# High and low activation parts as one 512-column moving operand in 39 projection units

## The chip, the cores and the metric

The kernel runs on one core of one Trainium2 chip. The metric is the device time of one execution in microseconds (us); three runs of the kernel before have a median of 1357.82 us (1357.82 to 1359.32).

## What is computed

The reference is two transformer-like blocks over 256 tokens of width 1024, in float32. Only the parts that the change touches are shown:

```python
# first block
h = rms_norm(x, g_pre_mix) * (1 + scale1) + shift1
(sc_b, sc_c, sc_x, q, k, v, z, xbc, dt_raw, gl_a, gl_b, gl_c) = split_columns(h @ w_in)
y_a = short_conv_mixer(sc_b, sc_c, sc_x, sc_conv_w) @ w_sc_out      # conv(sc_c * sc_x) * sc_b
y_b = stick_breaking_attention(q, k, v) @ w_sb_out
y_c = mamba2_mixer(z, xbc, dt_raw, ...) @ w_ssm_out                 # conv over xbc, then a scan
merged = sigmoid(gl_a) * y_a + sigmoid(gl_b) * y_b + sigmoid(gl_c) * y_c
x = x + gate1 * rms_norm(merged @ w_o, g_post_mix)
gt, up = jnp.split(h2 @ w_ffn_in, 2, axis=-1)
f = (silu(gt) * up) @ w_ffn_out
# second block
q, k, v, u = jnp.split(h @ w_in, ...)     # dilated attention on q, k, v; pooling on u
x = x + g1 * (concat([attn, pool]) @ w_out)
x = x + g2 * peer_ffn(h2, ...)            # 16384 experts, all evaluated densely here
```

## The kernel before, in words

**Split arithmetic.** Every projection multiplies weights by activations in a 32-bit format of reduced precision (`fp32r`). Both operands are split in a high part and the rest, and a product is the sum of three: weight high by activation high, weight high by activation low, weight low by activation high (`mm3`, lines 378 to 381). The activations stand in `hh` and `hl`, 8 chunks (k) of 128 channels by 256 tokens each.

**A unit.** Weights come in units of 1 MB (256 output columns): one DMA into a tile `raw`, then for each of the two halves s of 128 columns ScalarE casts the high part (`h`, line 148) and VectorE subtracts to get the low part (`l`, line 149). `raw`, `h` and `l` each have three buffers and a fourth that every fourth tile takes, so a load waits until VectorE has read the tile that held its buffer. `fm_steps` (line 383 on) runs a unit: for each half 8 chunks of three matmuls, 48 in all, each with 256 moving columns, into one PSUM tile of the tag `mm` that holds both halves. There are two `mm` tiles, which all units share in turn. The caller then evicts both halves at once: the gate columns with a ScalarE copy (line 631), `sc_c` with a ScalarE copy (line 658), q, k and u of the second block with ScalarE copies (lines 985, 988, 997); the feed-forward with a silu on ScalarE and a multiplication on VectorE that read PSUM (lines 935 and 936).

**Other work on VectorE and ScalarE.** Beside the units run a conditioning product with the weights `mod_w` and `w_ada` (VectorE, line 171, two instructions of 1024 columns for a load of 1 MB; `side()` hands one load to each unit of the first stage), in the first block the convolution of `xbc` (`conv`, lines 614 and 617, six chunks), the short convolution, both mixers, and in the second block the pooling and the softmax (`scores`). Every engine works through its instructions in a fixed order, which a scheduler sets when the program is built. The code steers it with `tc.issue_after(ins)`: what is written under it comes after `ins`. `hold["gate"]` keeps the eviction of the last unit for that purpose:

```python
    sc_c()
    with tc.issue_after(hold["gate"].ins):
        conv(4)
    ...
    with tc.issue_after(hold["gate"].ins):
        conv(0)
    sc_x()
    with tc.issue_after(hold["gate"].ins):
        conv(2)
```

**Stages of the program**, with their times in the trace: input projection by chunks to 65 us; v, `sc_c`, `sc_x` and 12 gate units woven with the mixers (the gate stage) to 203.8 us; `w_o` and a norm to 248 us; the feed-forward (10 steps of two input units and one output unit) to 424 us; a norm; u, q, k and scores of the second block from 445.6 to 485 us; attention and `w_out` to 518 us; then the dense expert part to the end, which uses `fm_steps` and is not rewritten.

Of the kernel before, what the change touches and what calls it, by code (L numbers as in the profile page):

```python
# [7 lines left out]
F32 = mybir.dt.float32  # L8
F32R = mybir.dt.float32r
# [4 lines left out]
AF = mybir.ActivationFunctionType  # L14
ALU = mybir.AluOpType
# [26 lines left out]
def kernel(ctx: ExitStack, tc: tile.TileContext, a: dict, out: bass.AP):  # L42
    nc = tc.nc
    mm = nc.tensor.matmul
    V, S, G = nc.vector, nc.scalar, nc.gpsimd

    const = ctx.enter_context(tc.tile_pool(name="const", bufs=1))
    pers = ctx.enter_context(tc.tile_pool(name="pers", bufs=1))
# [56 lines left out]
    cb = {}  # L105
    modp = {}

    def load_c(i, pool, tag="cb"):
        cb[i] = pool.tile([P, D], F32, tag=tag, name=f"cb{i}{tag}")
        src = a["c_2" if i else "c"]  # L110
        nc.sync.dma_start(cb[i], bass.AP(tensor=src.tensor, offset=src.offset, ap=[[0, P], [1, D]]))
        S.activation(cb[i], cb[i], AF.Silu)
# [208 lines left out]
    def residual_norm(acc, gb, normed, affine, xt, name, ws):  # L321


        got = []
        hh = pers.tile([P, KC, T], F32R, tag="hh", name="hh" + name)
        hl = pers.tile([P, KC, T], F32R, tag="hl", name="hl" + name)
        scale, shift = affine
        def start(c):
            gm[c], rn[c] = gated(c, acc[c], gb, normed, "r" + name, xt[c])
# [162 lines left out]
    for hs in HALF:  # L492
        pt = mmtile(f"pc{hs.start}")
        mm(pt, ones1[0:1, :], crow[:, hs], start=True, stop=True)
        with tc.issue_after(sq.ins):
            S.activation(cb[0][:, hs], pt, AF.Silu)
    hh = pers.tile([P, KC, T], F32R, tag="hh", name="hhn1")
    hl = pers.tile([P, KC, T], F32R, tag="hl", name="hln1")
    coef = work.tile([P, 8], F32, tag="cf", name="cf1", bufs=4)
    acc = [t.rearrange("p (s t) -> p s t", s=2) for t in  # L500
           [mmtile(f"acc_j{n}") for n in range(2)] + [attile(f"acc_i{n}") for n in range(6)]]
# [123 lines left out]
    sgs = {}  # L625

    def gate_unit(n):
        b, u = divmod(n, 4)
        if u == 0:
            sgs[b] = w1.tile([P, KC, T], F32, tag="sg", name=f"sg{b}", bufs=2)  # L630
        hold["gate"] = S.copy(sgs[b][:, 2 * u:2 * u + 2], fm_unit(W, 2 + n, hh, hl, f"gl{b}{u}"))

    def branch(b, src, yh, yl, kn):
        S.activation(sgs[b], sgs[b], AF.Sigmoid)
# [20 lines left out]
    scc = w1.tile([P, 2, T], F32, name="scc")  # L655

    def sc_c():
        hold["gate"] = S.copy(scc, fm_unit(W, 0, hh, hl, "scc"))

    def sc_x():  # L660
        hold["gate"] = V.tensor_tensor(upad[:, :, 2:], fm_unit(W, 1, hh, hl, "scx"), scc, op=ALU.mult)
# [252 lines left out]
    for u in range(11):  # L914
# [11 lines left out]
            continue  # L926
        fh = r2(f"fh{u}")
        for k in range(2):
            pt = fm_unit(a["w_ffn_in"], 2 * u + k, hh, hl, f"fi{u}{k}")
            for _ in range(1 + (k == 1 and u in (3, 6))):  # L930
                with after(u - 1):
                    mod_run()
                mod_load(*next(mods))
            sl = w0.tile([P, T], F32, tag="sl", name=f"sl{u}{k}", bufs=2)
            S.activation(sl, pt[:, 0], AF.Silu)
            later_than[u] = V.tensor_tensor(fh[:, k], pt[:, 1], sl, op=ALU.mult)
        if u == 1:
            pt = attile("pft").rearrange("p (k t) -> p k t", k=2)
            for c in range(2):
# [42 lines left out]
    cat = w2.tile([P, KC, T], F32, tag="cat", name="cat")  # L982

    def q_unit(u):
        S.copy(qf[:, 2 * u:2 * u + 2], fm_unit(W, u, hh, hl, f"q2{u}"))

    def k_unit(u):
        S.copy(kf[:, 2 * u:2 * u + 2], fm_unit(W, 2 + u, hh, hl, f"k2{u}"))

    def v_units():  # L990
        pv = [mmtile(f"pv2{c}") for c in range(2)]
# [2 lines left out]
            S.copy(vf[:, c], pv[c])  # L994

    def up_unit(u):
        S.copy(up[:, 2 * u:2 * u + 2, 16:], fm_unit(W, 4 + u, hh, hl, f"u2{u}"))


    es, pos = {}, {}  # L1000
# [309 lines left out]
    woven(1, range(NU - NB, NU), v_steps)  # L1310
    b4.close()
    more.update(pool=ctx.enter_context(tc.tile_pool(name="more2", bufs=1)), tags=("wh", "wl"))
    fin = pers.tile([P, 2, D], F32, tag="hl", name="fin")
    gb, fg = fin[:, 0], fin[:, 1]
    load_c(1, pers, "hh")
    S.dma_start(fg, bass.AP(tensor=a["final_g_2"].tensor, offset=a["final_g_2"].offset, ap=[[0, P], [1, D]]))
    for u in range(32, 62):
        if u in (33, 36, 39, 42):
# [8 lines left out]
    v_unit(62, 63)  # L1327


    gm = pers.tile([P, 2, D], F32, tag="hh", name="gm")  # L1330
    for c in range(2):
        o = gm[:, c]
        gated(c, acc[c], gb, False, "ry", None, o)
# [92 lines left out]
```

## Time and profile before

| | |
|---|---|
| runs, median of 3 | 1357.82 us |
| profiled execution, its own time | 1358.11 us |
| span of its trace | 1356.1 us |
| TensorE clock granted, mean | 0.989 |
| TensorE (PE) busy | 1309.2 us, 97% |
| VectorE (DVE) busy | 1032.9 us, 76% |
| ScalarE (ACT) busy | 651.2 us, 48% |
| HBM read | 281 MB |

In the rows that follow, PE is TensorE's matmuls, PEld its weight loads, DVE VectorE, ACT ScalarE, POOL GpSimd, SPq the queue that starts most DMAs. L149 is line 149 of the kernel before. A tile is named after the unit: `pgl` is the PSUM tile of a gate unit, `hgl` and `lgl` the high and low parts of its weights, `rgl` the loaded tile; `pscc` and `pscx` are the PSUM tiles of `sc_c` and `sc_x`; `pfi`, `hfi`, `lfi` belong to the feed-forward input. A busy time of a matmul is longer than its share of the array, since matmuls are pipelined; the distance between starts is what counts.

### The profile page before, as it was taken

The page shows a single profiled execution, that of the slowest core. Times are in us where ns is not written, and L with a number is a line of the kernel's source. Part 1 is how long each engine was busy: PE and PEld are TensorE (multiplying, and loading weights), DVE is VectorE, ACT ScalarE, POOL GpSimd, SP SyncE. Part 2 cuts the span into 40 slices and gives each one's busy share as a digit, 9 for nine tenths or more (in the row PEclk, how much of TensorE's full clock was granted, in tenths as well). Part 3 has the DMA queues.
Part 4 walks back from the last instruction along what each step waited for, and adds up shares of the span by engine and source line. Part 5 has one row for each costly group of instructions (what it writes and reads, how often), then busy time and mean ns, then how long its engine had stood idle before and what let it go on. Part 6 is the DMA issues. An engine that isn't in the chain of part 4 may idle for free.

```text
span 1356.1 us, 23558 instructions
## 1 busy us (share of the span) xinstructions
PE 1309.2 (97%) x9601; PEld 1200.8 (89%) x9601; DVE 1032.9 (76%) x1908; ACT 651.2 (48%) x838; POOL 121.9 (9%) x109
## 2 busy tenths in 40 slices
PE   7999998999998999998999999999999999999996
PEld 6999997999996988998999999999998888888885
DVE  6899876787986885758858688886447999865555
ACT  5576554544444564444445433434444443445443
POOL 0000002000002002544442000000000000000001
PEclk9999998999999999999999999999999999999999
DMA  8866574888875542444445544444555444676551
GB/s 346 341 249 249 220 268 150 308 321 338 334 305 233 188 170 97 157 178 151 152 176 185 187 156 156 164 170 168 186 190 213 160 182 156 239 261 229 186 188 60
DMA packets 41454, 283.64 MB, mean 209 GB/s; under 512 B 5041, under 2 KB 5377, under 8 KB 8194
## 3 DMA queue, kind: packets, MB, share of 16 engines
q1 hardware_dynamic: 40768, 281.12, 56.0%
q8 instruction: 75, 1.23, 0.4%
q10 hardware_dynamic: 578, 1.02, 0.2%
q14 instruction: 33, 0.27, 0.1%
HBM read 281.03 MB, written 1.09 MB: 208 GB/s over the span
## 4 chain that ended last, share of the span: by engine, by line
PE 85%; DVE 8%; ACT 3%; POOL 2%; issue 1%; DMA 0%; POOLq 0%; SPq 0%; ACTq 0%; DVEq 0%
PE acc_y L431 25%; PE pU L379 8%; PE pU L381 8%; PE pU L380 8%; PE acc_f L431 4%; PE pfi L380 3%; PE pfi L381 3%; PE pfi L379 3%; PE pw L1157 2%; PE pgl L379 1%; PE pgl L381 1%; PE pgl L380 1%; PE acc L431 1%; PE acc_o L431 1%; DVE mod L171 1%
## 5 line engine op out<-in xcount | busy, mean ns | idle before, releaser
L381 PE MATMUL pU<-hhn,lU 128*128 128x256 f32 x1024 | 291.1, 284 | 6.4 <-DVE lU L149 5.8
L379 PE MATMUL pU<-hhn,hU 128*128 128x256 f32 x1024 | 293.9, 287 | 1.9 <-ACT g L1121 1.0
L380 PE MATMUL pU<-hln,hU 128*128 128x256 f32 x1024 | 290.4, 284 | 0.0
L148 ACT CAST hU<-rU 128x1024 fp32r<-128x1024 f32 x128 | 133.9, 1049 | 212.7 <-PE pU L380 179.6
L148 ACT CAST hV<-rV 128x1024 fp32r<-128x1024 f32 x128 | 134.8, 1053 | 195.7 <-PE acc_y L431 151.8
L149 DVE TENSOR_TENSOR lV<-rV,hV 128x1024 fp32r<-128x1024 f32 x128 | 156.5, 1223 | 89.2 <-ACT hV L148 89.2
L149 DVE TENSOR_TENSOR lU<-rU,hU 128x1024 fp32r<-128x1024 f32 x105 | 131.7, 1256 | 98.1 <-ACT hU L148 98.1
L381 PEld LDWEIGHTS pU<-hhn,lU 128*128 128x128 f32 x1024 | 197.0, 192 | 7.6 <-DVE lU L149 6.6
L431 PE MATMUL acc_y<-hV,hP 128*128 128x512 f32 x512 | 202.0, 395 | 0.0
L431 PE MATMUL acc_y<-hV,lP 128*128 128x512 f32 x512 | 199.6, 390 | 0.0
L379 PEld LDWEIGHTS pU<-hhn,hU 128*128 128x128 f32 x1024 | 197.0, 192 | 2.6 <-ACT g L1121 1.2
L431 PE MATMUL acc_y<-lV,hP 128*128 128x512 f32 x512 | 199.3, 389 | 0.0
L380 PEld LDWEIGHTS pU<-hln,hU 128*128 128x128 f32 x1024 | 197.2, 193 | 0.3
L431 PEld LDWEIGHTS acc_y<-lV,hP 128*128 128x128 f32 x512 | 96.1, 188 | 19.9
L431 PEld LDWEIGHTS acc_y<-hV,lP 128*128 128x128 f32 x512 | 96.3, 188 | 18.9 <-DVE lP L375 0.4
L431 PEld LDWEIGHTS acc_y<-hV,hP 128*128 128x128 f32 x512 | 96.2, 188 | 18.9
L379 PE MATMUL pfi<-hhn,hfi 128*128 128x256 f32 x320 | 90.6, 283 | 0.0
L380 PE MATMUL pfi<-hln,hfi 128*128 128x256 f32 x320 | 90.5, 283 | 0.0
L381 PE MATMUL pfi<-hhn,lfi 128*128 128x256 f32 x320 | 90.5, 283 | 0.0
L148 ACT CAST hfi<-rfi 128x1024 fp32r<-128x1024 f32 x43 | 45.1, 1050 | 54.5 <-PE pfi L380 20.8
L149 DVE TENSOR_TENSOR lfi<-rfi,hfi 128x1024 fp32r<-128x1024 f32 x43 | 52.0, 1223 | 24.3 <-ACT hfi L148 24.2
L379 PEld LDWEIGHTS pfi<-hhn,hfi 128*128 128x128 f32 x320 | 61.4, 192 | 0.4
(538 smaller groups left out, 2869.8 us busy)
## 6 DMA issues: line engine op xcount, KB each, us to landing
rU<-in_peer_u_dram SPq DMA_DIRECT2D x64, 1024.0 KB, 4.8
rV<-in_peer_v_dram SPq DMA_DIRECT2D x64, 1024.0 KB, 4.8
mod<-in_mod_w_dram SPq DMA_DIRECT2D x24, 1024.0 KB, 6.0
mod<-in_w_ada_dram SPq DMA_DIRECT2D x24, 1024.0 KB, 5.0
rfi<-in_w_ffn_in_dram SPq DMA_DIRECT2D x22, 1024.0 KB, 7.3
rgl<-in_w_in_dram SPq DMA_DIRECT2D x12, 1024.0 KB, 4.8
rfo<-in_w_ffn_out_dram SPq DMA_DIRECT2D x11, 1024.0 KB, 8.3
rwq<-in_peer_wq_dram SPq DMA_DIRECT2D x8, 1024.0 KB, 4.9
```

Of the source, the lines that this page charges most:

```text
L148: S.copy(h, r)
L149: hold["l"] = (G if pool_lo and s else V).tensor_tensor(l, r, h.bitcast(F32), op=ALU.subtract)
L171: V.scalar_tensor_tensor(t[:, s], t[:, s], 1.0, cb[i], op0=ALU.mult, op1=ALU.mult, accum_out=mod[:, i, n:n + 1])
L379: mm(o, wh, ah, start=start, stop=False, skip_group_check=skip)
L380: mm(o, wh, al, start=False, stop=False, skip_group_check=skip)
L381: mm(o, wl, ah, start=False, stop=stop, skip_group_check=skip)
L431: mm(acc[c][b], st[:, k, tk], w[:, HALF[b]], start=start and k == 0 and n == 0, stop=stop and k == 1 and n == 2)
L1157: mm(pw[:, t], oa[:, q, :, r], og[:, i, q, :, r], start=(i == 0), stop=(i == 1))
```

## The change

`hh` and `hl` become the two halves of one tile `hw` of [128, 8, 2, 256]. A new function `fm_sums` takes the place of `fm_steps` in 39 units: 12 gate units, `sc_c`, 20 feed-forward input units, and two each of q, k and u. For each half and chunk it issues one matmul of 512 moving columns (weight high by activation high and low side by side) and one of 256 (weight low by activation high), 32 matmuls a unit. Each half has an `mm` tile of its own: its columns 256 to 511 hold weight high by activation low, columns 0 to 255 the sum of the other two products. To evict a half, ScalarE copies columns 256 to 511 to the destination in SBUF, and VectorE adds columns 0 to 255 to it. `hold["gate"]` is now that addition. `sc_x` and the expert part keep `fm_steps`. The feed-forward evicts into a tile `fp` and applies silu and the multiplication there. The last buffers (`fin`, `gm`, the second use of `cb`) move into the tag `hw`.

```diff
+    def fm_sums(src, u, dst, name, pool_lo=False):
+        side()
+        for s, h, l in weights(src, u, name, pool_lo):
+            pt = mmtile(f"p{name}{s}")
+            h = h.rearrange("p (k n) -> p k n", k=KC)
+            l = l.rearrange("p (k n) -> p k n", k=KC)
+            for k in range(KC):
+                def wide(stop):
+                    mm(pt, h[:, k], hw["t"][:, k].rearrange("p z t -> p (z t)"), start=k == 0, stop=stop,
+                       skip_group_check=True)
+
+                if k == 0:
+                    wide(False)
+                mm(pt[:, :T], l[:, k], hw["t"][:, k, 0], start=False, stop=False, skip_group_check=True)
+                if k:
+                    wide(k == KC - 1)
+            S.copy(dst[:, s], pt[:, T:])
+            hold["gate"] = V.tensor_tensor(dst[:, s], pt[:, :T], dst[:, s], op=ALU.add)
+            yield s
...
-        hold["gate"] = S.copy(sgs[b][:, 2 * u:2 * u + 2], fm_unit(W, 2 + n, hh, hl, f"gl{b}{u}"))
+        list(fm_sums(W, 2 + n, sgs[b][:, 2 * u:2 * u + 2], f"gl{b}{u}"))
...
-        hold["gate"] = S.copy(scc, fm_unit(W, 0, hh, hl, "scc"))
+        list(fm_sums(W, 0, scc, "scc"))
...
-            pt = fm_unit(a["w_ffn_in"], 2 * u + k, hh, hl, f"fi{u}{k}")
+            pt = r2(f"fp{u}{k}")
+            list(fm_sums(a["w_ffn_in"], 2 * u + k, pt, f"fi{u}{k}"))
...
-            sl = w0.tile([P, T], F32, tag="sl", name=f"sl{u}{k}", bufs=2)
-            S.activation(sl, pt[:, 0], AF.Silu)
-            later_than[u] = V.tensor_tensor(fh[:, k], pt[:, 1], sl, op=ALU.mult)
+            S.activation(pt[:, 0], pt[:, 0], AF.Silu)
+            later_than[u] = V.tensor_tensor(fh[:, k], pt[:, 1], pt[:, 0], op=ALU.mult)
...
-        S.copy(qf[:, 2 * u:2 * u + 2], fm_unit(W, u, hh, hl, f"q2{u}"))
+        list(fm_sums(W, u, qf[:, 2 * u:2 * u + 2], f"q2{u}"))
```

The built order changes with it. In the rows of the change line numbers are those of the changed file: L422 is the addition, L421 the copy, L413 the wide matmul, L418 the narrow one, L641 and L644 are `conv`, L178 the conditioning product, L149 the low part of weights.

VectorE at the head of the gate stage, before: chunks of `conv` (L614, L617) stand ahead of and around the low parts for `sc_c` (`lscc`), four of the six by the time that `sc_x` is begun.

```order
L614 TENSOR_SCALAR xbc<-xpad,vec 128x256 x2
L617 SCALAR_TENSOR_TENSOR xbc<-xpad,vec,xbc 128x256 x4
L149 TENSOR_TENSOR lscc_859<-rscc,hscc_858 128x1024
L617 SCALAR_TENSOR_TENSOR xbc<-xpad,vec,xbc 128x256
L614 TENSOR_SCALAR xbc<-xpad,vec 128x256
L617 SCALAR_TENSOR_TENSOR xbc<-xpad,vec,xbc 128x256 x2
L149 TENSOR_TENSOR lscc_887<-rscc,hscc_886 128x1024
```

VectorE at the same place, with the change: the additions of the two halves of `sc_c` (`pscc_860`, `pscc_883`), and what follows the second.

```order
L422 TENSOR_TENSOR scc<-pscc_860,scc 128x256
L178 SCALAR_TENSOR_TENSOR mod_10_1082,mod<-mod_10_1082,cb_162 128x1024
L149 TENSOR_TENSOR lgl_1024<-rgl_1021,hgl_1023 128x1024
L422 TENSOR_TENSOR scc<-pscc_883,scc 128x256
L641 TENSOR_SCALAR xbc<-xpad,vec 128x256 x2
L644 SCALAR_TENSOR_TENSOR xbc<-xpad,vec,xbc 128x256 x6
```

The last two rows stand there twice in a row (four chunks), then comes this, where `lgl_1047` is the low part for the second half of the first gate unit, `lgl_1087` and `lgl_1110` those of the second unit:

```order
L688 TENSOR_TENSOR upad<-pscx,scc 128x2x256
L641 TENSOR_SCALAR xbc<-xpad,vec 128x256 x2
L644 SCALAR_TENSOR_TENSOR xbc<-xpad,vec,xbc 128x256 x6
L149 TENSOR_TENSOR lgl_1047<-rgl_1021,hgl_1046 128x1024
L149 TENSOR_TENSOR lgl_1087<-rgl_1084,hgl_1086 128x1024
L149 TENSOR_TENSOR lgl_1110<-rgl_1084,hgl_1109 128x1024
L624 TENSOR_SCALAR dtt<-dtt 128x16
L178 SCALAR_TENSOR_TENSOR mod_10_1082,mod<-mod_10_1082,cb_162 128x1024
```

All six chunks of `conv` now follow the addition of `sc_c`'s second half and precede the low part of the first gate unit's second half. Behind these rows come two more L178, then the stick-breaking mixer's `lk` (L723, two), `zz` (L724, two) and the masking of `lk` (L726, two for each pair of heads).

VectorE there, with the change, from the masking for the second pair on; `sg_1016<-pgl_1027` and `sg_1016<-pgl_1050` are the additions of the first gate unit's two halves.

```order
L726 SCALAR_TENSOR_TENSOR lk<-lk,trius 128x2x256
L726 SCALAR_TENSOR_TENSOR lk<-lk,trius 128x2x128
L422 TENSOR_TENSOR sg_1016<-pgl_1027,sg_1016 128x256
L422 TENSOR_TENSOR sg_1016<-pgl_1050,sg_1016 128x256
L692 TENSOR_SCALAR scc<-upad,vec 128x256 x2
L694 SCALAR_TENSOR_TENSOR scc<-upad,vec,scc 128x256 x4
```

The two additions stand behind the mixer's eight instructions; before, a ScalarE copy emptied the tile and VectorE had no part in it.

TensorE at the same place, with the change; `pr` is the mixer's product with `lk`, `pgl_1090` the first half of the second gate unit, which takes the `mm` tile of `pgl_1027`.

```order
L418 MATMUL pgl_1050<-hwn_169,lgl_1047 128x256
L413 MATMUL pgl_1050<-hwn_169,hgl_1046 128x512
L732 MATMUL pr_1210<-lk,trils 128x256
L733 MATMUL pr_1210<-lk,ones_85 128x128
L413 MATMUL pgl_1090<-hwn_169,hgl_1086 128x512
L418 MATMUL pgl_1090<-hwn_169,lgl_1087 128x256 x2
```

The first `pr` now follows one gate unit; before, it followed two and a half.

## Rows read from the trace of the kernel before

**Rows 1.** The page's busy times: engine, share of the span, instructions.

```profile
PE 1309.2 (97%) x9601; PEld 1200.8 (89%) x9601; DVE 1032.9 (76%) x1908; ACT 651.2 (48%) x838; POOL 121.9 (9%) x109
```

**Rows 2.** Busy time by stretch: stretch, length, busy of each engine, clock, DMA share, GB/s.

```profile
62.36:80.00 17.64, 17.64 (x149) 16.82 (x148) 16.84 (x33) 10.46 (x18) 0.00 (x0) 1.00 0.57 211
80.00:104.40 24.40, 22.86 (x190) 22.32 (x190) 23.87 (x52) 20.04 (x22) 0.00 (x0) 1.00 0.62 237
104.40:178.47 74.07, 72.43 (x605) 69.71 (x604) 68.96 (x137) 42.14 (x48) 1.93 (x1) 1.00 0.68 256
178.47:203.80 25.33, 24.44 (x191) 24.18 (x192) 18.40 (x21) 12.71 (x15) 0.00 (x0) 0.93 0.67 240
248.00:424.00 176.00, 175.97 (x1231) 164.94 (x1230) 142.35 (x206) 80.56 (x103) 1.51 (x4) 1.00 0.87 338
445.60:485.00 39.40, 39.24 (x314) 38.03 (x313) 34.61 (x77) 23.13 (x34) 0.00 (x0) 1.00 0.49 180
```

**Rows 3.** The same view for `pfi` alone, then `acc_f` alone, in one feed-forward step.

```profile
299.92:311.43 11.51, 11.51 (x96) 11.46 (x95) 0.42 (x1) 0.38 (x1) 1.00 0.82 309
...
311.43:316.89 5.46, 5.46 (x24) 4.32 (x24) 0.00 (x0) 0.00 (x0) 1.00 0.99 419
```

**Rows 4.** Groups by line and shape, evictions: count, busy us, mean ns, idle before.

```profile
L936 DVE TENSOR_TENSOR fh<-pfi,sl 128x256 f32<-128x256 f32 x20 | 8.4, 418 | 0.1
...
L935 ACT ACTIVATE sl<-pfi 128x256 f32<-128x256 f32 x20 | 7.6, 378 | 0.0
...
L631 ACT COPY sg<-pgl 128x512 f32<-128x512 f32 x12 | 7.0, 584 | 17.2 <-PE pgl L381 17.2
```

**Rows 5.** VectorE's timeline in the gate stage: start, us, engine, line, operation.

```profile
60.08 2.36 DVE L149 TENSOR_TENSOR lv<-rv,hv 128x1024 fp32r<-128x1024 f32 x2 [0.52 <-ACT hv L148]
62.36 0.73 DVE L614 TENSOR_SCALAR xbc<-xpad,vec 128x256 f32<-128x256 f32 x2
...
87.11 0.73 DVE L614 TENSOR_SCALAR xbc<-xpad,vec 128x256 f32<-128x256 f32 x2
87.75 2.46 DVE L617 SCALAR_TENSOR_TENSOR xbc<-xpad,vec,xbc 128x256 f32<-128x256 f32 x6
90.13 0.61 DVE L665 TENSOR_SCALAR scc<-upad,vec 128x256 f32<-128x256 f32 x2
...
99.04 1.83 DVE L696 SCALAR_TENSOR_TENSOR lk<-zz,tt 128x768 f32<-128x768 f32 x2
...
102.52 1.96 DVE L699 SCALAR_TENSOR_TENSOR lk<-lk,trius 128x512 f32<-128x512 f32 x4
104.40 0.68 DVE L375 TENSOR_TENSOR lya<-scb,hya 128x512 fp32r<-128x512 f32 x1
...
119.96 1.22 DVE L171 SCALAR_TENSOR_TENSOR mod<-mod,cb 128x1024 f32<-128x1024 f32 x1
121.10 0.08 DVE L171 DVE_READ_ACCUMULATOR mod<-mod,cb 128x1 f32 x1
```

**Rows 6.** ScalarE's timeline in the gate stage, same columns.

```profile
88.17 1.49 ACT L691 ACTIVATE tt<-zz 128x1536 f32<-128x1536 f32 x1
89.68 1.28 ACT L621 ACT_TABLE_LOAD   x1
90.97 1.49 ACT L621 ACTIVATE xbc<-xbc 128x1536 f32<-128x1536 f32 x1
```

**Rows 7.** TensorE's timeline in the gate stage, same columns.

```profile
79.58 0.28 PE L381 MATMUL pscc<-hhn,lscc 128*128 128x256 f32 x1
...
103.57 0.28 PE L380 MATMUL pgl<-hln,hgl 128*128 128x256 f32 x1
...
179.74 0.39 PE L381 MATMUL pgl<-hhn,lgl 128*128 128x256 f32 x1 [0.66 <-DVE lgl L149]
```

**Rows 8.** DMA issues: count, KB each, median us to landing.

```profile
rgl<-in_w_in_dram SPq DMA_DIRECT2D x12, 1024.0 KB, 4.8
```

More of the change, by code (lines that the diff above doesn't have):

```diff
@@ L108, in load_c @@
     def load_c(i, pool, tag="cb"):
-        cb[i] = pool.tile([P, D], F32, tag=tag, name=f"cb{i}{tag}")
+        cb[i] = pool.tile([P, D], F32, tag=tag, name=f"cb{i}{tag}") if pool else gm[:, 0]
         src = a["c_2" if i else "c"]
@@ L150, in weights, with both @@
             yield s, h, l
+    hw = {}
+    def both(name):
+        hw["t"] = t = pers.tile([P, KC, 2, T], F32R, tag="hw", name="hw" + name)
+        return t[:, :, 0], t[:, :, 1]
     mod = const.tile([P, 2, 48], F32, name="mod")
@@ L324, in residual_norm @@
         got = []
-        hh = pers.tile([P, KC, T], F32R, tag="hh", name="hh" + name)
-        hl = pers.tile([P, KC, T], F32R, tag="hl", name="hl" + name)
+        hh, hl = both(name)
         scale, shift = affine
@@ L496 @@
             S.activation(cb[0][:, hs], pt, AF.Silu)
-    hh = pers.tile([P, KC, T], F32R, tag="hh", name="hhn1")
-    hl = pers.tile([P, KC, T], F32R, tag="hl", name="hln1")
+    hh, hl = both("n1")
     coef = work.tile([P, 8], F32, tag="cf", name="cf1", bufs=4)
@@ L984, in q_unit @@
     def q_unit(u):
-        S.copy(qf[:, 2 * u:2 * u + 2], fm_unit(W, u, hh, hl, f"q2{u}"))
+        list(fm_sums(W, u, qf[:, 2 * u:2 * u + 2], f"q2{u}"))
     def k_unit(u):
-        S.copy(kf[:, 2 * u:2 * u + 2], fm_unit(W, 2 + u, hh, hl, f"k2{u}"))
+        list(fm_sums(W, 2 + u, kf[:, 2 * u:2 * u + 2], f"k2{u}"))
     def v_units():
@@ L996, in up_unit @@
     def up_unit(u):
-        S.copy(up[:, 2 * u:2 * u + 2, 16:], fm_unit(W, 4 + u, hh, hl, f"u2{u}"))
+        list(fm_sums(W, 4 + u, up[:, 2 * u:2 * u + 2, 16:], f"u2{u}"))
     es, pos = {}, {}
@@ L1312 @@
     more.update(pool=ctx.enter_context(tc.tile_pool(name="more2", bufs=1)), tags=("wh", "wl"))
-    fin = pers.tile([P, 2, D], F32, tag="hl", name="fin")
-    gb, fg = fin[:, 0], fin[:, 1]
-    load_c(1, pers, "hh")
+    fin = pers.tile([P, 4, D], F32, tag="hw", name="fin")
+    gb, fg, gm = fin[:, 0], fin[:, 1], fin[:, 2:4]
+    load_c(1, None, "cb")
     S.dma_start(fg, bass.AP(tensor=a["final_g_2"].tensor, offset=a["final_g_2"].offset, ap=[[0, P], [1, D]]))
@@ L1327 @@
     v_unit(62, 63)
-    gm = pers.tile([P, 2, D], F32, tag="hh", name="gm")
     for c in range(2):
```

## The prediction

> **What bounds the kernel now.** The page's busy times come first [rows 1]: TensorE is busy 97% of the span, VectorE 76%, ScalarE 48%. So matmul time removed is time removed wherever TensorE alone sets the pace. That is a mean, so the windows come next [rows 2]. In the feed-forward and in the stretch of u, q, k and scores TensorE is busy all but 0.2 us and VectorE has 34 and 5 us free. In the gate stage both are full: from 62.36 to 178.47 VectorE is idle 0.80 + 0.53 + 5.11 = 6.4 us in 116.1. Extra VectorE work is cheap in the former stretches and dear in the latter. For the gate stage I then read the three engines' timelines [rows 5 to 7] against the built order.
>
> The sum is made against the profiled execution's own 1358.11 us, 0.3 above the median of the runs shown. A measurement of this kernel can tell about 0.2% (2.7 us) from no change, so "same" is 1355.1 to 1360.5.
>
> **What TensorE saves.** `pfi` takes 119.9 ns for a matmul of 256 columns, `acc_f` 227.5 ns for one of 512 [rows 3]. Two of the former become one of the latter: 239.8 - 227.5 = 12.3 ns saved, 16 times a unit, 0.197 us. For 39 units that is 7.7 us at most: 3.9 in 20 feed-forward units, 1.2 in six of q, k and u, 2.6 in 13 of the gate stage. Columns stay; only the fixed part of a matmul goes.
>
> The Trainium skill puts that part lower: "TensorE: Matmul & The Clock Gate", section "Back-to-back issue gap", gives columns / 2.4 GHz plus 2.5 ns for an isolated matmul, so that merging two saves 2.5 ns, an estimate of 1.6 us for all 624. The rows show 13 and 14 ns above columns / 2.4 GHz, not 2.5, and the measurement decides.
>
> **What is added.** For each half a ScalarE copy of 128x256 from PSUM, nearest row 0.378 us, and a VectorE addition, nearest row 0.418 us [rows 4]; consecutive VectorE instructions overlap by about 0.08 (the next starts 1.14 after a start with 1.22 busy, rows 5), so I take 0.34 of VectorE's time. A unit costs VectorE 0.68 and ScalarE 0.756 instead of 0.584 [rows 4]. A half's tile is free after copy and addition, 0.8 us behind its last matmul if neither queues. The two `mm` tiles now hold one half each, so TensorE runs at most about one half (2.8 us) ahead of an addition; before, a tile held a whole unit and VectorE had no part in freeing it.
>
> **The gate stage.** The built order puts all six `conv` chunks behind the addition of `sc_c`'s second half, where before four lay ahead of `sc_x`. `sc_c` ended at 79.58 [rows 7]. TensorE is two shortened halves earlier, so copy and addition of the second half end at about 80.4. What VectorE has ahead of it makes some 11.8 us, from 62.36 on where `conv` began [rows 5], in 17.6 us: 5.9 idle where 0.80 was.
>
> From 80.4 VectorE works in order: four chunks, 6.0 (two take 3.02, from 87.11 to 90.13, rows 5); `upad` 0.6; two chunks 3.0, to 90.1; `lgl_1047` and two further low parts, 1.14 each (two start at 60.08 and end by 62.36, rows 5), to 93.5; three conditioning products of 1.14 and small ones, to 97.3. ScalarE's absolute value, table load and silu on `xbc`, 1.3 to 1.5 us each [rows 6], end by then and add nothing. `lk`, `zz` and the first masking take 5.36 - 0.94 = 4.4, since from 99.04 to 104.40 both maskings are in it [rows 5]. So the first `pr` can start at 101.8 and the second masking ends at 102.7. Only then comes the addition of `pgl_1027`, to 103.1, which frees the tile for the second gate unit.
>
> TensorE meanwhile ends `sc_x` near 87.0, the first gate unit's first half 2.8 later, waits for `lgl_1047` to 91.3, ends the second half at 93.9, and then stands **idle to about 103.1, some 9 us**. Before, 122 of the 144 matmuls of three gate units were done by 103.57 [rows 7], now the 32 of one unit.
>
> Can it catch up? VectorE's own work says no. From 62.36 to 178.47 it did 116.1 - 6.4 = 109.7 us; 22 additions (2 of `sc_c`, 20 of ten gate units) make it 117.2. By 103.4 it has done 41.0 - 6.1 = 34.9, so 82.3 remain: 185.7, and with the low part of gate unit 10 (1.14) TensorE resumes at 186.9, where before it resumed 0.4 to 0.7 before 180 [rows 7], I take 179.6. The floor is **+7.3 us**, with no idle left on VectorE. Two further waits I can name: 1.4 near 123, where ScalarE's copy of a gate half stands behind a table load and an activation (1.28 + 1.49, rows 6) of which about half is uncovered; 2.3 where the load of gate unit 5 waits for a buffer that a conditioning product reads only behind an addition, and then takes 4.8 to land [rows 8]. That makes 11.0; the last two gate units are PE-bound and give back 0.4: **+10.6**. Bounds: +6.9 (no such waits) to +13 (two more of about a microsecond at the mixers' products). A stall of TensorE may also cost clock: the stretch in which it resumed at 179.74 ran at a granted 0.93 [rows 2]; that loss of up to 1.8 us was there before, and I put nothing more on it.
>
> **The feed-forward.** A step is two such units and an output unit, 16.6 us after the change. VectorE had 142.35 / 10 = 14.2 us of work in it [rows 2] and gets 1.36, 15.6 of 16.6: still free. The weights, 338 GB/s over the whole stretch [rows 2], would come 2% faster; a stretch of `acc_f` shows 419 [rows 3]. An addition may stand behind a conditioning product or a low part (1.14), and the tile is needed one half (2.6 us) later, so it is covered; if that cover goes, up to 0.3 a step is lost, 3 us. I take -3.9, and +0.4 at the last step, where copy, addition and silu stand one after another before the last output unit: **-3.5** (-4 to 0).
>
> **q, k and u.** VectorE gets 12 additions, 4.1 us, with 34.61 of 39.40 busy [rows 2]: nearly full. I take **-1.0** of 1.2 (bounds -1.2 and +1). `w_o`, norms, attention and the expert part keep their instructions and only shift.
>
> **Sum:** 1358.1 + 10.6 - 3.5 - 1.0 = 1364.2, forecast **1364.0 us**; with the gate stage's bounds 1360.5 to 1366.6, and to 1371 if the feed-forward and q, k and u take their worse bounds too.
>
> **The rivals.**
> 1. *VectorE's idle time takes the additions (faster).* Place: its queue from 62 to 178. If what precedes the second addition of `sc_c` fills the time to 80, the lag at 103 does not arise, and only 7.5 of additions against 6.4 of idle time are left: +1.1, less 0.4. 1358.1 + 0.7 - 4.5 = 1354.3. For it: TensorE was busy 72.43 of 74.07 there [rows 2], with low parts ahead. Against: the built order, by which `conv` cannot begin before 80. It decides from a gate-stage loss below 1.8 on. Chance 0.09.
> 2. *The loss is only half as large (no change).* The lag is 5 instead of 9, since VectorE's rows hold waits on ScalarE that vanish when it is late, and later idle time absorbs part: +4.5, 1358.1. Chance 0.15.
> 3. *The feed-forward gains nothing.* Additions behind conditioning products hold a tile too long in every step: 3.5 lost of the sum, 1367.7, up to 1371. For it: two tiles of half the reach; against: 1 us free a step. Chance 0.11.
> 4. *Columns alone set TensorE's pace.* Then merging gives nothing: The gate stage loses 11.0, as units 10 and 11 give nothing back, the feed-forward the 0.4 of its uncovered end, q, k and u 0.2 of waits: 1369.7. Against: 13 ns fixed at either width [rows 3], though no row has wide and narrow matmuls in turn. Chance 0.05. The formula of the Trainium skill quoted above (same page and section) comes near this case.
>
> The forecast keeps 0.60. Its own range is 1360.5 to 1368. **Range**: rival 2 and the upper bounds belong in, rival 1 and the far tails (about 0.17) stay out: 1356.5 to 1371. **Chances:** faster 0.09 (rival 1); same 0.16 (rival 2 and the lowest edge of the forecast); slower 0.75.
>
> **What the profile afterwards should show.** VectorE idle about 6 us before 80, waiting for the copy of `pscc`. TensorE idle some 9 us between 94 and 103, released by an addition of `sg` or by `lk`. VectorE idle under 3 us from 104 to gate unit 10, which begins near 190, and `acc_o` near 214 instead of 203.8. `pfi` in 11.1 us instead of 11.51, the feed-forward 172.5 instead of 176, the stretch of u, q, k one shorter. If TensorE's idle time in the gate stage is under 5 us in all, the forecast is wrong on VectorE; if a wide matmul and a narrow one take 359 ns together instead of 347, it is wrong on what merging saves; if the feed-forward has gaps at each first matmul of a half, on the tiles.

## The result and the profile after

The changed kernel takes **1368.5 us** (median of 4 runs, 1368.03 to 1370.02) beside 1357.82 us before: a ratio of 1.008, with a 95% interval of 1.0068 to 1.0091. It is slower, as forecast; the time lies inside the range of 1356.5 to 1371.0 and 4.5 us above the forecast of 1364.0.

The page's busy times, of the changed kernel (its span is 1366.0 us, 9.9 longer than before):

```profile
PE 1309.7 (96%) x8977; PEld 1170.3 (86%) x8977; DVE 1058.6 (77%) x1986; ACT 664.0 (49%) x896; POOL 120.1 (9%) x109
```

There are 624 matmuls fewer than before [rows 1], yet TensorE is busy for the same 1309 us, at a mean granted clock of 0.985 instead of 0.989, and idle for 56.3 instead of 46.9 us (span less busy). Busy shares say little here, so stages are compared by the distance from one landmark to the next (starts of matmuls, us). acc_o is `w_o`, pfi the first feed-forward unit, acc_f the output units, pu the first unit of the second block's `u`, acc `w_out`, pU the first expert unit.

| stage | before | after | difference |
|---|---|---|---|
| start to first acc_o (gate stage) | 203.80 | 212.61 | +8.8 |
| to first pfi | 44.34 | 44.31 | 0 |
| to last acc_f (feed-forward) | 176.16 | 172.69 | -3.5 |
| to first pu (norm, v) | 21.38 | 22.79 | +1.4 |
| to last acc (u, q, k, attention) | 72.51 | 73.05 | +0.5 |
| to first pU (norm, query weights) | 13.61 | 16.17 | +2.6 |
| to last matmul (experts) | 813.69 | 813.65 | 0 |

The sum is +9.8. The forecast had +10.6, -3.5 and -1.0 for the first, third and fifth row and nothing for the others.

Windows of the changed kernel, columns as in [rows 2]:

```profile
62.36:80.00 17.64, 17.64 (x135) 16.09 (x134) 12.06 (x18) 10.79 (x20) 0.00 (x0) 1.00 0.73 276
80.00:104.40 24.40, 16.03 (x101) 13.85 (x100) 24.40 (x53) 15.69 (x18) 0.00 (x0) 0.89 0.51 190
104.40:178.47 74.07, 73.32 (x473) 63.51 (x472) 68.53 (x148) 41.99 (x56) 1.93 (x1) 0.99 0.56 206
...
256.91:429.60 172.69, 172.69 (x911) 147.41 (x910) 156.85 (x245) 92.75 (x142) 1.24 (x4) 1.00 0.87 338
```

VectorE is idle for 17.64 - 12.06 = 5.6 us ahead of 80, then busy without a gap, while TensorE is busy 16.03 of 24.40. From 104.40 on VectorE is idle for 74.07 - 68.53 = 5.5 us, about as much as before (5.1 by [rows 2]).

VectorE's timeline at the head of the gate stage, changed kernel:

```profile
77.37 0.43 DVE L422 TENSOR_TENSOR scc<-pscc,scc 128x256 f32<-128x256 f32 x1 [2.06 <-ACT scc L421]
...
80.05 0.42 DVE L422 TENSOR_TENSOR scc<-pscc,scc 128x256 f32<-128x256 f32 x1
80.40 0.73 DVE L641 TENSOR_SCALAR xbc<-xpad,vec 128x256 f32<-128x256 f32 x2
...
97.17 1.83 DVE L723 SCALAR_TENSOR_TENSOR lk<-zz,tt 128x768 f32<-128x768 f32 x2
...
100.64 1.97 DVE L726 SCALAR_TENSOR_TENSOR lk<-lk,trius 128x512 f32<-128x512 f32 x4
102.51 0.76 DVE L422 TENSOR_TENSOR sg<-pgl,sg 128x256 f32<-128x256 f32 x2
```

and TensorE's there:

```profile
93.80 0.39 PE L413 MATMUL pgl<-hwn,hgl 128*128 128x512 f32 x1
101.39 1.22 PE L732 MATMUL pr<-lk,trils 128*128 128x256 f32 x2 [7.20 <-DVE lk L726]
102.41 0.64 PE L733 MATMUL pr<-lk,ones 128*128 128x128 f32 x2
103.00 0.80 PE L413 MATMUL pgl<-hwn,hgl 128*128 128x512 f32 x1
```

The last matmul of the first gate unit starts at 93.80. Both `mm` tiles are full then, and their additions stand behind `lk` and its masking: nothing for TensorE to do until `pr` at 101.39, and no gate unit before 103.00. The first `pr` even comes 2.3 us earlier than before (103.69); what is missing are one and a half gate units that lay ahead of it. Behind this idle time TensorE's granted clock fell: it is 0.89 in the mean from 80 to 104.40, and the second gate unit began at the lower of the two levels (1.2 of 2.4 GHz), without a gap:

```profile
103.00:106.03 3.03, 3.03 (x11) 2.65 (x11) 3.03 (x9) 0.00 (x0) 0.00 (x0) 0.50 0.30 124
```

One feed-forward step, the stretch of its two input units and of its output unit:

```profile
307.80:318.98 11.18, 11.18 (x65) 9.76 (x64) 8.89 (x13) 5.75 (x9) 0.00 (x0) 1.00 0.97 381
318.98:324.43 5.45, 5.45 (x26) 4.51 (x24) 5.42 (x9) 2.99 (x4) 0.00 (x0) 1.00 1.00 419
```

11.18 us for 32 pairs is 349 ns for a wide and a narrow matmul, where three narrow ones took 360 (11.51 in rows 3): 10.3 ns saved by each merge.

### The profile page after: what moved, and what is told of

The parts are those of the page before. It is cut to its first block, busy times and chain, and to the rows that moved or that the text cites. A ratio compares the mean times of both kernels' runs of the same rounds, so it can differ in the third digit from the quotient of the medians.

```text
span 1366.0 us, 22375 instructions
## 1 busy us (share of the span) xinstructions
PE 1309.7 (96%) x8977; PEld 1170.3 (86%) x8977; DVE 1058.6 (77%) x1986; ACT 664.0 (49%) x896; POOL 120.1 (9%) x109
## 4 chain that ended last, share of the span: by engine, by line
PE 84%; DVE 7%; ACT 2%; issue 2%; POOL 2%; DMA 1%; POOLq 0%; SPq 0%; ACTq 0%; DVEq 0%
PE acc_y L459 25%; PE pU L385 8%; PE pU L387 8%; PE pU L386 8%; PE pfi L413 5%; PE acc_f L459 4%; PE pgl L413 3%; PE pfi L418 3%; PE pw L1184 2%; DVE mod L178 2%; PE pgl L418 1%; PE acc L459 1%; PE acc_o L459 1%; PE pwq L386 1%; PE pwq L385 1%
## 5 line engine op out<-in xcount | busy, mean ns | idle before, releaser
L387 PE MATMUL pU<-hwn,lU 128*128 128x256 f32 x1024 | 291.6, 285 | 6.2 <-DVE lU L149 5.8
L385 PE MATMUL pU<-hwn,hU 128*128 128x256 f32 x1024 | 294.4, 288 | 1.9 <-ACT g L1148 1.0
L386 PE MATMUL pU<-hwn,hU 128*128 128x256 f32 x1024 | 291.1, 284 | 0.0
L149 DVE TENSOR_TENSOR lV<-rV,hV 128x1024 fp32r<-128x1024 f32 x128 | 156.5, 1224 | 89.2 <-ACT hV L148 89.1
L149 DVE TENSOR_TENSOR lU<-rU,hU 128x1024 fp32r<-128x1024 f32 x105 | 131.7, 1257 | 98.0 <-ACT hU L148 97.9
L387 PEld LDWEIGHTS pU<-hwn,lU 128*128 128x128 f32 x1024 | 197.3, 193 | 7.4 <-DVE lU L149 6.6
L385 PEld LDWEIGHTS pU<-hwn,hU 128*128 128x128 f32 x1024 | 197.3, 193 | 2.6 <-ACT g L1148 1.2
L386 PEld LDWEIGHTS pU<-hwn,hU 128*128 128x128 f32 x1024 | 197.5, 193 | 0.3
L413 PE MATMUL pfi<-hwn,hfi 128*128 128x512 f32 x320 | 111.3, 397 | 0.0
L418 PE MATMUL pfi<-hwn,lfi 128*128 128x256 f32 x320 | 82.8, 279 | 0.0
L413 PE MATMUL pgl<-hwn,hgl 128*128 128x512 f32 x192 | 69.0, 406 | 2.8 <-ACT hgl L148 2.8
L413 PEld LDWEIGHTS pfi<-hwn,hfi 128*128 128x128 f32 x320 | 58.1, 188 | 11.4 <-DVE fp L422 0.2
L418 PEld LDWEIGHTS pfi<-hwn,lfi 128*128 128x128 f32 x320 | 60.4, 189 | 3.4
L1187 DVE SCALAR_TENSOR_TENSOR g<-pw,g 128x368 f32<-128x368 f32 (+1 forms) x96 | 46.1, 509 | 19.5 <-PE pw L1184 19.0
```

The lines of the kernel that those rows point to most:

```text
L385: mm(o, wh, ah, start=start, stop=False, skip_group_check=skip)
L386: mm(o, wh, al, start=False, stop=False, skip_group_check=skip)
L387: mm(o, wl, ah, start=False, stop=stop, skip_group_check=skip)
L413: mm(pt, h[:, k], hw["t"][:, k].rearrange("p z t -> p (z t)"), start=k == 0, stop=stop, skip_group_check=True)
L418: mm(pt[:, :T], l[:, k], hw["t"][:, k, 0], start=False, stop=False, skip_group_check=True)
L1187: V.scalar_tensor_tensor(g, pw[:, :, j0:j0 + n].rearrange("p t j -> p j t"), 1.0 / GS, g, op0=ALU.mult, op1=ALU.mult)
```

## The experiments

In all of them what is not named is as in the kernel before in its built order; the shared buffer `hw` alone leaves that order unchanged on all engines. Each ratio is to the kernel before, measured in the same session; e5 to e8 ran on another chip than the rest.

**The change in three parts.** `e1_gate_only` keeps the new code in the 13 units of the gate stage, `e2_ffn_only` in the 20 of the feed-forward, `e3_qku_only` in the six of q, k and u. The edit, for instance in e2:

```diff
-        list(fm_sums(W, 2 + n, sgs[b][:, 2 * u:2 * u + 2], f"gl{b}{u}"))
+        hold["gate"] = S.copy(sgs[b][:, 2 * u:2 * u + 2], fm_unit(W, 2 + n, hh, hl, f"gl{b}{u}"))
...
-        list(fm_sums(W, u, qf[:, 2 * u:2 * u + 2], f"q2{u}"))
+        S.copy(qf[:, 2 * u:2 * u + 2], fm_unit(W, u, hh, hl, f"q2{u}"))
```

> Only the 12 gate units and sc_c are rewritten; feed-forward, q, k and u as before. Theory (the parts add up, and the gate stage loses on VectorE's queue): acc_o starts 8.8 us later than before, as in the change (212.6 against 203.8), the built order of the norms behind the feed-forward and behind w_out is that of before, so nothing is added there: span 1364.9, 8.8 above before, ratio about 1.0065. Rival (the late gate stage also disturbs the later stages, for instance by late loads): the later stages, too, grow by some 3 us, and the ratio is about 1.009.

> Only the 20 feed-forward input units are rewritten. Theory: the feed-forward is shorter by 3.5 us (176.2 to 172.7 from the first pfi to the last acc_f), and the norm behind it is longer by 1.4, since the built order leaves 13 instead of 20 matmuls of acc_f behind the last one of the first 128 tokens, so less work covers that norm's start: 2.1 faster, about 1355.8, ratio 0.9985. Rival (the 1.4 comes from the late gate stage or from q, k, u): the norm keeps its 21.4 us and the kernel gains 3.5.

> Only q, k and u of the second block are rewritten. Theory: the stretch from the first pu to the last matmul of acc loses about 0.5, and the stretch from there to the first pU loses about 2.5, because the built order of the norm behind w_out is another one (8 instead of 12 or more matmuls are left when the first 128 tokens are done, and VectorE takes the second half's products first): about 3 slower, 1361, ratio 1.002. Rival (additions cost nothing here, fewer matmuls pay): 1 us faster, 1357, ratio 0.999.

| | ratio (95% interval) | gate stage | feed-forward | norm, v | u to acc | norm, query weights |
|---|---|---|---|---|---|---|
| e1 | 1.0073 (1.0059 to 1.0087) | +8.9 | 0 | +1.6 | 0 | 0 |
| e2 | 0.9987 (0.9978 to 0.9996) | 0 | -3.2 | +1.4 | +0.8 | 0 |
| e3 | 1.0017 (1.0008 to 1.0026) | -1.4 | 0 | 0 | +0.5 | +2.2 |

(us against the profile of before.) The parts account for the whole: the gate stage loses 8.9, the feed-forward gains 3.2 and costs 1.4 behind it, and q, k and u lose in their own stretch and in the norm behind it. (The 0.8 of e2 from u on is for the most part one wait of TensorE for VectorE's `e` of the scores, 1.1 us instead of 0.4; e8, with the same feed-forward, has 0.4 there.) The first rival, that the late gate stage disturbs the later stages by late loads, falls; but e1 has 1.6 in the norm that the theory did not expect, with the order of before. The windows of e1 there, before and behind the start of the norm's last transpositions:

```profile
433.08:447.16 14.08, 7.90 (x31) 5.69 (x29) 10.73 (x16) 4.46 (x13) 7.88 (x12) 0.88 0.10 30
447.16:456.09 8.93, 8.93 (x36) 7.45 (x37) 7.27 (x13) 3.86 (x6) 0.00 (x0) 0.81 0.44 161
```

and the same two stretches of the kernel before:

```profile
424.30:438.38 14.08, 8.03 (x31) 5.60 (x29) 10.74 (x16) 4.46 (x13) 7.88 (x12) 0.88 0.10 35
438.38:445.68 7.30, 7.30 (x37) 6.13 (x38) 6.60 (x13) 3.87 (x6) 0.00 (x0) 1.00 0.36 128
```

The first stretch is equal to a hundredth; the second ran at a granted clock of 0.81 instead of 1.00 behind it, and took 1.6 longer. So a stage can cost 1.6 us by the clock alone, with the same instructions. It depends on where the lower level falls: in e5 and e6 below, again in the order of before, the first 14.08 us ran at 0.76 and the rest at 1.00, and the norm took 21.4, since TensorE has idle time in the first stretch anyway. The -1.4 of e3 in the gate stage, with the instructions of before, goes with the clock too: from 178.47 to 203.80 it was 1.00 in e3 and 0.93 before [rows 2]. And e6 and e8 below, with the same edit in that stage, are 2.7 apart in it. So a single trace tells the gate stage to two or three microseconds; the verdicts rest on the timed ratios, and the stages tell where.

**Where the norm behind the feed-forward grows.** Its 22.8 us in the changed kernel and in e2 are not the clock's. Up to the start of the last transpositions, 0.9 us behind the VectorE scaling that releases them, as before, they take 14.30 us in the changed kernel (14.08 before); the rest, all at a granted 1.00, takes 8.48 instead of 7.30:

```profile
443.91:452.39 8.48, 8.43 (x39) 6.75 (x40) 8.06 (x12) 3.87 (x6) 0.00 (x0) 1.00 0.58 209
```

Of the 48 matmuls of `pv` in that stage, 31 stand behind the last transpositions, and 28 before the change: three fewer fill TensorE's idle time ahead of them. At 0.23 us each that is 0.7 of the 1.2; the rest was not followed up.

**Where e3 loses.** In the changed kernel and in e3 the built order of `w_out` leaves the first 128 tokens complete later, and VectorE takes the second half's products ahead of the first half's scaling. GpSimd's chain for the first 128 tokens in the kernel before, where the last matmul of `acc` starts at 518.19:

```profile
517.03 0.29 POOL L253 TENSOR_SCALAR rt_n<-msxrn 128x1 f32<-128x1 f32 x1 [79.59 <-ACT gmrn L264]
```

and in the changed kernel, where it starts at 525.45:

```profile
525.42 1.07 POOL L260 TENSOR_SCALAR rt_n<-msxrn 128x1 f32<-128x1 f32 x1 [82.44 <-ACT gmrn L271]
```

It begins 1.16 us ahead of that matmul before and 0.03 ahead now, 1.1 later, and its first instruction took 0.8 longer, so that the first transpositions start 1.9 us later. The scaling for the second half starts only 0.3 later, though (7.70 us behind the matmul instead of 7.39). Its transpositions could then start 0.9 us behind it, as before, at 8.6; they start at 10.89, 2.6 later than before, because TensorE is still at work on the query weights of the first half, at a lower clock. The stretch ahead of them, before and with the change:

```profile
523.17:526.48 3.31, 2.99 (x20) 2.82 (x18) 2.30 (x5) 0.59 (x1) 2.08 (x4) 0.75 0.00 0
```

```profile
531.44:536.34 4.90, 4.90 (x26) 4.90 (x25) 2.51 (x4) 0.59 (x1) 1.47 (x3) 0.52 0.02 5
```

TensorE had stood idle for 3.5 us behind the last matmul of `acc` when the clock fell, and for 1.6 before. At the 0.12 us that a matmul of the query weights takes at the upper level, 23 of them take 2.8 instead of 4.9 us: by this estimate the clock makes some 2 of the 2.6 us. No run has the late start without the lower clock.

**The order of conv, and who frees a tile.** Four kernels with the gate stage alone:

```diff
# e4_gate_hold_copy
-            S.copy(dst[:, s], pt[:, T:])
-            hold["gate"] = V.tensor_tensor(dst[:, s], pt[:, :T], dst[:, s], op=ALU.add)
+            hold["gate"] = S.copy(dst[:, s], pt[:, T:])
+            V.tensor_tensor(dst[:, s], pt[:, :T], dst[:, s], op=ALU.add)
# e5_gate_copy_both (e6_gate_pool_add: G for V in the last line)
+            both = ev.tile([P, 2 * T], F32, tag="ev", name=f"ev{name}{s}", bufs=2)
+            hold["gate"] = S.copy(both, pt)
+            V.tensor_tensor(dst[:, s], both[:, :T], both[:, T:], op=ALU.add)
# e7_conv_order_only (projection units as before)
-        hold["gate"] = S.copy(scc, fm_unit(W, 0, hh, hl, "scc"))
+        S.copy(scc, fm_unit(W, 0, hh, hl, "scc"))
+        hold["gate"] = V.tensor_scalar(scc[:, 1, :1], scc[:, 1, :1], 1.0, None, op0=ALU.mult)
```

> As e1_gate_only, but hold["gate"] is the ScalarE copy instead of the VectorE addition, so that the chunks of conv stand ahead of and around the low parts of sc_c again, as before. Theory (the additions themselves block VectorE's queue: the one of sc_c waits for 80 with low parts and products behind it, and those of the first gate unit stand behind the mixer's lk, zz and masking, holding both mm tiles): conv's place matters little, acc_o starts 5 to 9 us later than before, ratio 1.004 to 1.0065. Rival (conv moved behind the addition is the cause): the loss falls below 3 us, ratio under 1.002.

> As e1_gate_only, but ScalarE copies all 512 columns of a half to an SBUF tile (two buffers), and VectorE adds the two halves of that tile. VectorE has the same 26 additions, but the mm tile is free after the ScalarE copy (0.58 us) whatever stands ahead of the addition; hold["gate"] is the copy. Theory (two costs: an mm tile held behind VectorE's queue, and VectorE's 22 further instructions up to gate unit 9, 7.5 us against 6.4 us of idle time): the first goes, the second stays, so that acc_o starts 1 to 5 us later than before, ratio 1.000 to 1.004. Rival (only VectorE's added work counts, who frees the tile is all the same): 6 us or more stay, as in e4_gate_hold_copy.

> As e5_gate_copy_both, but GpSimd makes the additions, so that VectorE's work is that of before. Theory (VectorE is the bound of the gate stage, TensorE's 2.6 us of saving come out once nothing is added to it): acc_o starts 1 to 2.6 us earlier than before, ratio 0.998 to 0.999. Rival (the additions cost by their accesses or by their own length, about 1 us on GpSimd, whichever engine makes them): no gain or a loss, ratio 1.000 or more.

> The kernel of before in all projection units, with one tiny VectorE instruction behind sc_c's eviction (one column of scc times 1), to which hold["gate"] points: the chunks of conv then stand behind sc_c on VectorE as in the change, without additions and with the tiles freed by ScalarE as before. Theory: the lag of about 5 us that VectorE gets ahead of 80 is for the most part made up by its 5.1 us of idle time after 104: acc_o starts 0 to 4 us later, ratio 1.000 to 1.003. Rival (conv's place is most of the loss): 6 us or more.

| | ratio (95% interval) | `pacs` later by | acc_o later by | TensorE's longest waits there |
|---|---|---|---|---|
| e1 | 1.0073 (1.0059 to 1.0087) | 8.8 | 8.9 | 7.2 on `lk` |
| e4 | 1.0049 (1.0035 to 1.0063) | 9.9 | 6.5 | 10.3 on `lk` |
| e5 | 1.0056 (1.0042 to 1.0070) | 4.8 | 7.3 | 4.3 on ScalarE's copy, 2.7 on `lgl` |
| e6 | 1.0050 (1.0036 to 1.0064) | 10.0 | 9.4 | 2.8 on ScalarE's copy, 2.7 on a norm's `rs_sg` |
| e7 | 1.0024 (1.0015 to 1.0033) | 6.6 | 3.7 | 1.8 on `lgl`, 5.0 in four waits |

(`pacs` is the Mamba mixer's first product, at 115.60 before.) e4 and e7 came as the theory had it: the additions alone, with `conv` where it was, cost 6.5 (by the ratio 6.7), and the place of `conv` alone, without an addition, costs 3.7 (by the ratio 3.3). Neither alone is the cause; together they cost 8.9 (by the ratio 9.9), a little less than their sum. e5 went to the rival: with the tiles freed by ScalarE `pr` has its gate units ahead of it again (65 matmuls of `pgl` from 87.16 to 105.71), but the additions and the longer copies delay the low and high parts of weights later on, and 7.3 remain (by the ratio 7.6, between 5.7 and 9.5). The 7.3 also hold lower clocks than before: 0.86 from 80 to 104.40, where it was 1.00 [rows 2]. e6 went to the rival too. GpSimd's additions slow VectorE down; e6's rows of `lk`, 768 columns each:

```profile
L728 DVE SCALAR_TENSOR_TENSOR lk<-zz,tt 128x768 f32<-128x768 f32 x2 | 2.4, 1214 | 0.0
...
L424 POOL TENSOR_TENSOR sg<-evgl 128x256 f32<-128x256 f32 x24 | 26.6, 1110 | 91.5 <-ACT evgl L423 91.5
```

Before they took a mean of 954 ns (1.83 us for two in rows 5). `lgl` up to 178 took a mean of 1326 ns in e6 and 1218 before: the 8 that overlap an instruction of GpSimd 1486, the other 12 1220. How much of e6's 9.4 us that is, and how much its waits on ScalarE's copies, is not shown.

**Is it VectorE's load?**

> As e1_gate_only, but of the conditioning products made in the gate stage (12 loads) every second instruction takes 128 of 1024 columns; the rest of those products is left out, the loads stay. That takes some 1.0 us 12 times, 12 us, from VectorE between 62 and 200. To be compared with e10_before_less_products. Theory (VectorE is the bound of the changed gate stage): acc_o starts 0 to 4 us later than in e10, since the 7.5 us of additions now find room and only the wait at 80 and the tile held behind lk remain. Rival (what holds TensorE is the path from matmul to copy to addition to matmul, not VectorE's load): acc_o stays 7 us or more behind e10.

> The kernel of before with the same part of the conditioning products left out as in e9. Theory (before, TensorE was within 2 us of its bound in the gate stage): acc_o starts at most 2.5 us earlier than 203.8. Rival (VectorE already set the pace before): 4 us or more earlier.

```diff
+            w = P if i == 0 and 8 <= u < 20 and s else D
-            V.scalar_tensor_tensor(t[:, s], t[:, s], 1.0, cb[i], op0=ALU.mult, op1=ALU.mult,
+            V.scalar_tensor_tensor(t[:, s, :w], t[:, s, :w], 1.0, cb[i][:, :w], op0=ALU.mult, op1=ALU.mult,
```

acc_o starts at 208.78 in e9 and at 199.95 in e10: **8.8 apart, as with the full products** (212.71 and 203.80). By its number the rival holds: some 11 us less of VectorE's work (12 instructions of 0.28 instead of 1.22 us) do not make the loss smaller, and `pr` comes no earlier (`pr` at 101.67, `pacs` at 124.47, in e1 101.63 and 124.40). The ratios agree within their intervals: 1.0042 (1.0027 to 1.0057) beside 0.9978 (0.9969 to 0.9987), 0.0064 apart where e1 stands 0.0073 above the kernel before. The kernel before gained 3.9 us of gate stage by it, more than the 2.5 expected. But e10 ran at a granted 1.00 from 178.47 to 203.80, as e3 did; beside e3's 202.43 it gains 2.5. e9's window from 80 to 104.40, where the loss arises:

```profile
80.00:104.40 24.40, 17.22 (x101) 14.69 (x100) 24.16 (x62) 15.67 (x18) 0.00 (x0) 0.83 0.49 187
```

VectorE is full there in spite of the shortened products: the order puts `conv`, low parts and mixer between the addition at 80 and the one that frees the tile. Of the shortened products only two stand between 80 and `lk`, and the order of e9 has eight more small instructions of `dtt` there than that of e1, so that `lk` starts at 97.45 as in e1 (97.41). So e9 shows that VectorE's work behind the head is not what keeps the loss; it did not make the head's queue shorter.

**Versions that gain.** `e8_pool_gate_ffn` joins e6 and e2; `e11_ffn18_q_k` rewrites the feed-forward's steps 1 to 8 (16 units) and q and k; `e12_gate10_11_ffn18_q_k` also the last two gate units.

```diff
# e11
-            pt = r2(f"fp{u}{k}")
-            list(fm_sums(a["w_ffn_in"], 2 * u + k, pt, f"fi{u}{k}"))
+            if u < 9:
+                pt = r2(f"fp{u}{k}")
+                list(fm_sums(a["w_ffn_in"], 2 * u + k, pt, f"fi{u}{k}"))
+            else:
+                pt = fm_unit(a["w_ffn_in"], 2 * u + k, hh, hl, f"fi{u}{k}")
# e12 besides
+        if n >= 10:
+            list(fm_sums(W, 2 + n, sgs[b][:, 2 * u:2 * u + 2], f"gl{b}{u}"))
+        else:
+            hold["gate"] = S.copy(sgs[b][:, 2 * u:2 * u + 2], fm_unit(W, 2 + n, hh, hl, f"gl{b}{u}"))
```

> The gate stage as in e6_gate_pool_add and the feed-forward as in e2_ffn_only; q, k and u as before. Theory: both gains add up, 1 to 2.6 us from the gate stage and 1.5 to 2.1 from the feed-forward with its norm: 1353.5 to 1355.5, ratio 0.9965 to 0.998. Rival (the gate stage gains nothing with GpSimd): as e2_ffn_only, ratio 0.9987, or above.

> The feed-forward's input units of steps 1 to 8 of 10 wait no more for the last step: only the first 16 of its 20 units are rewritten, and q and k of the second block; sc_c, gate units, the last four feed-forward units and u as before. Theory (the built order costs what the matmuls gain): with 17 matmuls of acc_f left to cover the norm instead of 13 in e2, the norm behind the feed-forward takes 21.4 to 22.3 us, the feed-forward itself about 173.2; the norm behind w_out is ordered as before (13.6 from the last acc to the first pU); q and k gain up to 0.8: together 3 faster, ratio 0.998. Rival (q and k lose to waits as in e3, and the norm is as long as in e2): ratio 0.9985 or more.

> As e11_ffn18_q_k, and gate units 10 and 11 rewritten, which lie where VectorE has free time (18.4 us of 25.3 busy). Theory: 0.4 more gained, acc_o starts 0.4 earlier, ratio 0.9975 to 0.998. Rival (additions behind other work hold tiles here too): acc_o starts later than in e11.

| | ratio (95% interval) | gate stage | feed-forward | norm, v | u to acc | norm, query weights |
|---|---|---|---|---|---|---|
| e8 | 1.0035 (1.0023 to 1.0048) | +6.8 | -3.3 | +1.4 | 0 | 0 |
| e11 | 0.9990 (0.9981 to 0.9999) | 0 | -2.6 | +1.7 | -0.9 | 0 |
| e12 | 0.9983 (0.9974 to 0.9991) | -0.3 | -2.5 | +1.8 | -1.1 | 0 |

e8 missed, as e6 did. In e11 q and k gain the 0.8 that their matmuls are worth, and the norm behind `w_out` keeps its length: in e3 it was `u`, which stands beside the pooling and the scores, that turned the gain into a loss. But by its ratio e11 went to the rival (0.9985 or more), for 17 instead of 13 matmuls behind the first tokens did not shorten the norm behind the feed-forward (23.1 us). Its last transpositions start earlier than before (13.76 us from the last acc_f, 14.08 before), but 36 matmuls of `pv` stand behind them instead of 28, and that rest takes 9.33 instead of 7.30 us. The two gate units of e12 gave 0.2 to 0.3 of the 0.4 expected. e12, with a median of 1355.70 beside 1358.12, has the lowest median of the complete kernels; its interval overlaps those of e2 and e11, and it beats the kernel before by little.

## Why the prediction was right, and where it was off

**TensorE's saving**: right in kind, a little too high. 12.3 ns were forecast for a merge and 10.3 measured. That the feed-forward came to -3.5 as forecast is in part luck: 320 merges of 10.3 ns make 3.3, not 3.9, and the 0.4 of the last step did not show there. By an estimate from the formula in the Trainium skill ("TensorE: Matmul & The Clock Gate", section "Back-to-back issue gap") a merge would save 2.5 ns; the trace does not agree.

**The head of the gate stage**: right step by step. VectorE idle 5.6 us ahead of 80 (forecast 5.9), `lk` at 97.17 (97.3), `pr` at 101.39 (101.8), the second gate unit at 103.00 (103.1). Only the idle time's reason was half right: 2.1 of the 5.6 us wait for the copy of `pscc`, 3.5 for the high parts of the weights of `sc_c` and `sc_x`. The clock, on which the prediction put nothing more, fell there: 3.03 us of full work at 0.50 from 103.00 on cost 1.5, by an estimate. The up to 1.8 that the kernel before lost near 180 was not lost again (1.00 from 124.10 on, below), so that leaving the clock out did no harm in the sum; that was luck.

**"Can it catch up? VectorE's own work says no"**: this step failed, though its size was near (+10.6 forecast, +8.8 measured). It took VectorE for full from 103 on and laid 3.7 us of waits on top. It had 5.5 us free, where the prediction put under 3, and e9 with e10 shows that less of its work there does not make the difference smaller. From `pacs` to acc_o the changed kernel took 88.5 us and the kernel before 88.2: nothing more was lost there, and nothing made up. The windows of before and of the change show why, 115.60 to 203.80 and 124.10 to 212.61:

```profile
115.60:203.80 88.20, 85.67 (x707) 82.85 (x706) 76.16 (x131) 49.76 (x59) 1.93 (x1) 0.98 0.69 255
```

```profile
124.10:212.61 88.51, 84.33 (x578) 74.37 (x576) 80.48 (x149) 50.18 (x65) 1.93 (x1) 1.00 0.61 226
```

TensorE had only 88.20 - 85.67 = 2.5 us free there before, so there was little to make lost time up from, and with the change 4.2. What 128 merges save (1.3 us at 10.3 ns) and what the clock gives back (0.98 before, 1.00 now) went into waits, of which 1.7 show as idle time. In other orders of the stage part was made up: in e4 the 9.9 at `pacs` are 6.5 at acc_o, in e7, which merges nothing, 6.6 are 3.7. Of the two waits named, that on a load came, at another unit (2.34 ahead of gate unit 10, behind the load's arrival); that on a copy behind a table load did not.

**"`w_o`, norms, attention and the expert part keep their instructions and only shift"**: this is the step that put the forecast 4 us low. They keep their instructions, not their order: the norm behind the feed-forward grew by 1.4 and that behind `w_out` by 2.6. Behind the feed-forward 13 matmuls of acc_f are left behind the first tokens' last one, and 20 before, in the built orders; yet that delays the last transpositions by 0.2 only. The other 1.2 stand behind them, where three more matmuls of `pv` are left. The lower clock at the norm's start (0.77 in e2, 0.76 in e8, 0.88 before) is not the cause: e5 and e6 have 0.76 there in the order of before, and 21.4 us. Behind `w_out` the 2.6 came by a later start and a longer stretch at the lower clock.

**q, k and u**: -1.0 forecast, +0.5 measured, within the bounds of -1.2 and +1 but of the other sign. e11 shows that q and k alone gain 0.9; `u` is what loses.

**The sum**: the gate stage was put 1.8 us too high, the norms 4.0 and q, k and u 1.5 too low, so that errors of opposite sign make part of the nearness. The stated worse bounds add up to 1358.1 + 13 + 0 + 1 = 1372.1, not 1371; the result lies below either.

**The rivals**: that VectorE's idle time takes the additions did not come about, as the order said; a gate-stage loss of 8.8 is not the half of the second rival, a feed-forward of -3.5 is not the nothing of the third, and that columns alone set the pace is excluded by 349 ns a pair. Why freeing the tiles by ScalarE (e5) left 7.3 us is only partly shown, by the waits on copies and low parts; it stays open how these divide between VectorE's additions, ScalarE's longer copies and the clock.

## What to carry to other kernels

Before a matmul is merged so that an eviction needs two engines, ask who frees the accumulator and what stands ahead of it in that engine's queue: here two tiles behind a queue of 20 us cost more than all merged matmuls saved. Where TensorE is nearly full afterwards, it has little room to make a wait up, even if the engine that caused it has time later. And a changed unit can move the built order of stages that were not edited: compare their orders too, above all how many matmuls are left to fill TensorE's idle time in each norm and how many stand behind its last transpositions.

## What the runs showed that was not expected

GpSimd's additions with two SBUF operands (1110 ns for 128x256) go with longer two-input instructions of VectorE in the same stretch (`lk` 1214 instead of 954 ns; `lgl` 1486 with an overlap, 1220 without), so work moved to an idle engine was paid for in part by the full one. The Trainium skill names this contention ("GPSIMD Engine Reference", section "1. Specifications": the SBUF interfaces are shared with VectorE, and VectorE's instructions with two SBUF inputs contend), and the trace agrees. A norm with the same instructions in the same order took 21.4 or 23.0 us, by a granted clock of 1.00 or 0.81 behind its last transpositions, while 0.76 instead of 0.88 ahead of them cost nothing: where the lower clock falls can cost as much as a small change is worth.
